# Encoder trunk in generator steps: one order list a layer, 512-column query/key projections, diff scores over 128 rows, norm and residual loads later

## The chip, the cores and the metric

The program runs on one core of one Trainium2 chip. A core has five engines with instruction queues of their own: TensorE (PE, matmuls; its weight loads are listed as PEld), VectorE (DVE), ScalarE (ACT), GpSimd (POOL) and SyncE (SP, which here only issues DMAs). The metric is the device time of one execution in microseconds (us). Before the change it is 1037.87 us, the median of three runs (1037.47 to 1038.59). All rows below come from one profiled execution of 1037.91 us, whose span from the first to the last instruction is 1035.7 us, so 2.2 us lie around the span; it stands 0.04 us from the median.

## The reference

Two layers of an encoder over 256 tokens of width 1024. Each layer projects x once into queries, keys, values and gates, runs three attention branches, merges them through sigmoid gates, and adds a feed-forward block. Cut to what matters:

```python
for l in range(DEPTH):                                   # DEPTH = 2
    h = x @ w_in[l]
    c_q, c_kv, k_pe, dq, dk, dv, mq, gate_pre = jnp.split(h, splits, axis=-1)
    o_mla  = _mla_branch(...)                            # 8 heads, low-rank q and kv
    o_diff = _diff_branch(dq, dk, dv, ...)               # 8 heads, two softmax maps each
    o_mem  = _mem_branch(mq, mem, mem_w_kv[l])           # 4 heads into 256 memory tokens
    merged = g0*(o_mla @ wb0) + g1*(o_diff @ wb1) + g2*(o_mem @ wb2)
    x = _layernorm(DEEPNORM_ALPHA * x + merged @ w_out[l], ln1_g[l], ln1_b[l])
    f = jnp.square(jax.nn.relu(x @ mlp_w1[l])) @ mlp_w2[l]
    x = _layernorm(DEEPNORM_ALPHA * x + f, ln2_g[l], ln2_b[l])

# diff branch: q, k are (b, s, 8 heads, 2 maps, 64); rope on the first 16 of 64
sc = jnp.einsum('bqhcd,bkhcd->bhcqk', qblk, k) * 64 ** -0.5
p  = softmax(sc);  w = p[:, :, 0] - lambda_full * p[:, :, 1];  o = w @ v
```

## The kernel before

Every operand of a matmul is split into a high and a low part, both in the type fp32r: `evac` (L129) writes the high part with ACT and the low part, the rest, with DVE, and `mm3` (L112) multiplies high x high, high x low and low x high as three matmuls into one PSUM tile. Weights come by `wload` (L93): one DMA of 512 KB on SP's queue into a `raw` tile, a cast on ACT (L104) and a subtraction on DVE (L105) into a `whl` tile. There are 6 `raw` and 8 `whl` tiles. PSUM has two rings of four tiles, `acc` and `sm`.

A layer is emitted as steps in the order of the string `ORDER` (L52). P0 to P3 are the diff projections of two heads each, D0 to D3 their attention, K, Q and M the memory branch, L, U and A the latent branch, g, h, e the gates and G, H, E the branch products. Then come `w_out`, a layer norm, the feed-forward block (`mlp1`, `mlp2`) and a second layer norm. A step is one Python call. The framework's scheduler then fixes each engine's order from all the instructions that were emitted; every engine runs its own queue strictly in that order and waits on semaphores.

The places that the change touches:

- `DiffProj` (L189) projects queries, keys and values of two heads as three pieces `i` of 256 columns each for two tiles `t` of 128 tokens. Queries and keys of a token tile share one PSUM tile, queries in columns 0 to 255 and keys in 256 to 511. `finish` copies that tile (L232), rotates it, transposes it (L240) and splits queries and keys with `evac` (L242).
- `diff_head` (L448) computes the scores of one head. A head has two maps of 64 dimensions, map 0 on partitions 0 to 63 and map 1 on 64 to 127, so each matmul (L458) uses 64 rows: 2 token tiles x 3 products x 2 maps, 12 a head, each over 256 columns. The two maps alternate.
- `ln_params` (L532) takes a `whl` tile for the norm's gain and bias; `xn` (L821) loads the residual. The second norm's load is emitted ahead of the feed-forward block (L862).
- For the first layer's P0 the kernel calls `first.both()` (L316): piece by piece, and within a piece both token tiles.

Of the kernel before, what the change touches and what calls it, by code (L numbers as in the profile page):

```python
# [43 lines left out]
BUFS = dict(raw=6, whl=8, whlx=4, att=12, o=6, pexp=4, natd=3, gt=4, fr=2, pT=2)  # L44
# [7 lines left out]
ORDER = "P0 T0 L0 K0 Q0 D0 U0 M0 P1 D1 M1 P2 D2 P3 g0 A0 G0 D3 g1 g2 A1 G1 A2 G2 g3 G3 h0 H0 h1 A3 h2 H1 e0 h3 H2 H3 e1 E0 e2 e3 E1 E2 E3"  # L52
CONST_W = 1700
# [3 lines left out]
def encoder_trunk(ctx: ExitStack, tc: tile.TileContext, x, mem, positions, w_in, b_gate,  # L57
# [34 lines left out]

    def wload(src, a, b, ring="whl"):  # L93
# [95 lines left out]
    class DiffProj:  # L189
# [12 lines left out]
        def proj(self, i, t):  # L202
            stage[0] = "diff_proj"
            if i == 2:
                if self.vv is None:
                    self.vv = acc_tile()
                d = self.vv[:, t * T:(t + 1) * T]
            else:
                if self.qk[t] is None:
                    self.qk[t] = acc_tile()  # L210
                d = self.qk[t][:, i * T:(i + 1) * T]
            for k in range(KD):
                w = self.weights(i, k // 4)
                xh, xl = xk(self.xT, k, t)
                mm3(d, xh, xl, w[0][:, k % 4], w[1][:, k % 4], k == 0, k == KD - 1)

        def step(self, t):
            for i in range(3):
                self.proj(i, t)

        def both(self):
            for i in range(3):
                for t in range(2):
                    self.proj(i, t)
            return self

        def finish(self):
            stage[0] = "diff_proj"
            nats = []
            for t in range(2):  # L230
# [39 lines left out]
    def mem_keys(l, mT, ptile):  # L270
        stage[0] = "mem_keys"
        K = []
        for hp in range(2):
            ws = [wload(wsrc(w_mkv[l], 4 * c, 4, hp * 256, 256), 4, 256) for c in range(2)]
# [12 lines left out]
        return K  # L287
# [28 lines left out]
    first.both()  # L316
# [112 lines left out]
    def attend_pair(q, k, rows):  # L429

        st = tmp.tile([P, 2, 2], F32, tag="st", bufs=4, name=nm("st"))
        pes = []
        for t in range(2):
            ps = sm_tile()
# [5 lines left out]
            pes.append(softmax_exp(ps, st, t))  # L440
        rc = tmp.tile([P, 2, 2], F32, tag="rc", bufs=4, name=nm("rc"))
# [4 lines left out]
        return [transpose_probs([pes[t][:, j, :] for t in range(2)]) for j in range(2)]  # L446

    def diff_head(l, q, k, j, vh, on):  # L448

        st = tmp.tile([P, 2, 2], F32, tag="st", bufs=4, name=nm("st"))  # L450
        pss = [sm_tile() for _ in range(2)]
        ks = slice(j * T, (j + 1) * T)
        for t in range(2):
# [6 lines left out]
        pes = [softmax_exp(pss[m], st, m) for m in range(2)]  # L460
        rc = tmp.tile([P, 2, 2], F32, tag="rc", bufs=4, name=nm("rc"))
# [4 lines left out]
        for t in range(2):  # L466
            V.scalar_tensor_tensor(pes[0][:, t, :], pes[1][:, t, :], rc[:, 1, t:t + 1], pes[0][:, t, :],
                                   ALU.mult, ALU.add)
        pT = transpose_probs([pes[0][:, t, :] for t in range(2)])
        po = sm_tile()  # L470
# [8 lines left out]
        ss = tmp.tile([P, 2], F32, tag="ss", bufs=4, name=nm("ss"))  # L479
        junk = tmp.tile([P, 384], F32, tag="junk", bufs=1, name=nm("junk"))  # L480
        for t in range(2):
            S.activation(junk[:, :P], on[:, t, :], AF.Square, accum_out=ss[:, t:t + 1])
        rs_ = tmp.tile([P, 2], F32, tag="rs", bufs=4, name=nm("rs"))
        G.tensor_tensor(rs_, ss, rc[:, 0, :], ALU.add)
        G.tensor_tensor(rs_, rs_, nhalf[:, :2], ALU.pow)
        for t in range(2):
            S.activation(on[:, t, :], on[:, t, :], AF.Copy, scale=rs_[:, t:t + 1])

# [8 lines left out]
    def relu_sq(ps):  # L497
        r = tmp.tile([P, 512], F32, tag="gt", bufs=BUFS["gt"], name=nm("relu"))
# [33 lines left out]
    def ln_params(g, b):  # L532
        gb = wp.tile([P, 2, D], F32, tag="whl", bufs=BUFS["whl"], name=nm("lnp"))
# [438 lines left out]
```

## Time and profile before

| What | Value |
|---|---|
| Median of three runs | 1037.87 us (1037.47 to 1038.59) |
| Profiled execution | 1037.91 us, span 1035.7 us |
| PE busy | 1018.0 us, 98% of the span, 6725 matmuls |
| PEld (weight loads) busy | 926.5 us, 89% |
| DVE busy | 723.6 us, 70% |
| ACT busy | 571.7 us, 55% |
| POOL busy | 54.6 us, 5% |
| DMA, main queue | 176.71 MB, 56.7% of 16 engines |
| Chain that ended last | PE 97%, DVE 1%, DMA 1% |

Busy time counts a moment once however many instructions of the engine are in flight then. Matmuls overlap: one is listed with 280 ns, while the next starts 120 ns behind it. What a matmul costs in a stream is therefore the distance from its start to the next start, and not its listed duration.

### The profile page before, as it was taken

Reading aid. Unit: us, or ns where it says so; the run is one execution under the profiler, and the core shown is the slowest. Engines: PE = TensorE matmul, PEld = TensorE weight load, DVE = VectorE, ACT = ScalarE, POOL = GpSimd, SP = SyncE. Lnnn points to the kernel's source line nnn. Section 1 sums busy time; section 2 is a strip of 40 time slices with the busy share of each in tenths; the row PEclk is TensorE's granted clock in tenths of the full one; section 3 lists DMA queues with packets and bytes.
Section 4 is the critical chain, followed back from the end, with each engine's and each line's share of the span. In section 5 each row is a group of like instructions: output and inputs, shape, how many; then the busy total and the mean of one; then the engine's idle time right before and its main releaser. Section 6 shows DMA issues by size and latency. Waiting matters only on the chain.

```text
span 1035.7 us, 17211 instructions
## 1 busy us (share of the span) xinstructions
PE 1018.0 (98%) x6725; PEld 926.5 (89%) x6725; DVE 723.6 (70%) x1095; ACT 571.7 (55%) x1054; POOL 54.6 (5%) x102
## 2 busy tenths in 40 slices
PE   7999999999999999999999999999999999999996
PEld 6989999999998888888889999999999978888885
DVE  5868778766869776556876777776677876556664
ACT  5857657657554554445625775666565625344540
POOL 0201000001000000000000210100000010000001
PEclk9999999999999999999999999999999999999999
DMA  8956444444558466666845864445455835755531
GB/s 295 337 161 173 134 123 145 141 123 125 173 181 274 143 203 190 193 187 183 252 128 186 237 163 124 133 132 142 122 147 160 265 122 166 240 163 183 183 102 41
DMA packets 132761, 178.11 MB, mean 172 GB/s; under 512 B 6028, under 2 KB 114632, under 8 KB 132680
## 3 DMA queue, kind: packets, MB, share of 16 engines
q1 hardware_dynamic: 132032, 176.71, 56.7%
q8 instruction: 53, 0.87, 0.4%
q10 hardware_dynamic: 648, 0.31, 0.1%
q14 instruction: 28, 0.23, 0.1%
HBM read 174.89 MB, written 2.10 MB: 171 GB/s over the span
## 4 chain that ended last, share of the span: by engine, by line
PE 97%; DVE 1%; DMA 1%; ACT 0%; SPq 0%; issue 0%; POOLq 0%; POOL 0%; DVEq 0%
PE mlp1.sm L121 11%; PE mlp2.acc L113 6%; PE mlp2.acc L115 6%; PE mlp2.acc L114 6%; PE mlp1.sm L123 5%; PE diff_proj.acc L113 5%; PE diff_proj.acc L114 5%; PE diff_proj.acc L115 5%; PE gate.acc L115 4%; PE gate.acc L113 4%; PE gate.acc L114 4%; PE branch.acc L114 4%; PE branch.acc L113 4%; PE branch.acc L115 4%; PE diff_att.sm L458 2%; PE diff_att.sm L474 2%
## 5 line engine op out<-in xcount | busy, mean ns | idle before, releaser
L105 DVE TENSOR_TENSOR mlp1.whl<-mlp1.raw,mlp1.whl 128x1024 fp32r<-128x1024 f32 x124 | 150.1, 1223 | 69.8 <-ACT mlp1.whl L104 67.8
L121 PE MATMUL mlp1.sm<-wout.xT,mlp1.whl 128*128 128x512 f32 x480 | 166.6, 397 | 0.0
L104 ACT CAST mlp1.whl<-mlp1.raw 128x1024 fp32r<-128x1024 f32 x124 | 127.8, 1049 | 62.2 <-PE mlp2.acc L115 23.6
L123 PE MATMUL mlp1.sm<-wout.xT,mlp1.whl 128*128 128x256 f32 x420 | 117.8, 280 | 0.0
L121 PEld LDWEIGHTS mlp1.sm<-wout.xT,mlp1.whl 128*128 128x128 f32 x480 | 87.0, 188 | 16.8
L113 PE MATMUL mlp2.acc<-mlp1.whl,mlp1.att 128*128 128x512 f32 x240 | 95.1, 396 | 0.0
L115 PE MATMUL mlp2.acc<-mlp1.whl,mlp1.att 128*128 128x512 f32 x240 | 94.2, 393 | 0.0
L114 PE MATMUL mlp2.acc<-mlp1.whl,mlp1.att 128*128 128x512 f32 x240 | 94.0, 392 | 0.0
L123 PEld LDWEIGHTS mlp1.sm<-wout.xT,mlp1.whl 128*128 128x128 f32 x420 | 79.3, 189 | 2.6
L105 DVE TENSOR_TENSOR gate.whl<-gate.raw,gate.whl 128x1024 fp32r<-128x1024 f32 x48 | 58.7, 1223 | 25.5 <-ACT gate.whl L104 24.0
L105 DVE TENSOR_TENSOR diff_proj.whl<-diff_proj.raw,diff_proj.whl 128x1024 fp32r<-128x1024 f32 x47 | 57.4, 1222 | 20.3 <-ACT diff_proj.whl L104 19.7
L494 ACT COPY mlp1.sum<-mlp1.sm 128x256 f32<-128x256 f32 x60 | 22.4, 373 | 87.2 <-PE mlp1.sm L121 87.2
L104 ACT CAST diff_proj.whl<-diff_proj.raw 128x1024 fp32r<-128x1024 f32 x47 | 49.3, 1050 | 27.0 <-PE diff_proj.acc L115 16.0
L104 ACT CAST gate.whl<-gate.raw 128x1024 fp32r<-128x1024 f32 x48 | 50.3, 1049 | 20.7 <-PE gate.acc L115 10.0
L113 PE MATMUL diff_proj.acc<-diff_proj.whl,mlp1.xT 128*128 128x256 f32 x192 | 54.8, 286 | 0.5 <-ACT mlp1.xT L131 0.5
L113 PE MATMUL gate.acc<-start.xT,gate.whl 128*128 128x256 f32 x192 | 55.0, 286 | 0.0
L113 PE MATMUL gate.acc<-mlp1.xT,gate.whl 128*128 128x256 f32 x192 | 55.0, 286 | 0.0
L115 PEld LDWEIGHTS mlp2.acc<-mlp1.whl,mlp1.att 128*128 128x128 f32 x240 | 45.1, 188 | 11.1
L114 PE MATMUL diff_proj.acc<-diff_proj.whl,mlp1.xT 128*128 128x256 f32 x192 | 55.0, 287 | 0.0
L115 PE MATMUL gate.acc<-start.xT,gate.whl 128*128 128x256 f32 x192 | 54.8, 285 | 0.0
L115 PE MATMUL gate.acc<-mlp1.xT,gate.whl 128*128 128x256 f32 x192 | 54.8, 285 | 0.0
L114 PE MATMUL gate.acc<-start.xT,gate.whl 128*128 128x256 f32 x192 | 54.6, 284 | 0.0
(360 smaller groups left out, 2952.1 us busy)
## 6 DMA issues: line engine op xcount, KB each, us to landing
mlp1.raw<-in_mlp_w_dram SPq DMA_DIRECT2D x124, 512.0 KB, 4.6
gate.raw<-in_w_in_dram SPq DMA_DIRECT2D x48, 512.0 KB, 3.8
diff_proj.raw<-in_w_in_dram SPq DMA_DIRECT2D x47, 512.0 KB, 4.6
branch.raw<-in_w_branch_dram SPq DMA_DIRECT2D x32, 512.0 KB, 3.6
wout.raw<-in_w_out_dram SPq DMA_DIRECT2D x16, 512.0 KB, 3.8
mem_keys.raw<-in_mem_w_kv_dram SPq DMA_DIRECT2D x8, 512.0 KB, 5.4
mem_vals.raw<-in_mem_w_kv_dram SPq DMA_DIRECT2D x8, 512.0 KB, 6.9
mq.raw<-in_w_in_dram SPq DMA_DIRECT2D x8, 512.0 KB, 5.4
```

The lines of the kernel that those rows point to most:

```text
L104: S.copy(out=hl[:, 0, :n], in_=raw[:, :n])
L105: V.tensor_tensor(hl[:, 1, :n], raw[:, :n], f32v(hl[:, 0, :n]), ALU.subtract)
L113: PE.matmul(ps, lhsT=lh, rhs=rh, start=start, stop=False)
L114: PE.matmul(ps, lhsT=lh, rhs=rl, start=False, stop=False)
L115: PE.matmul(ps, lhsT=ll, rhs=rh, start=False, stop=stop)
L121: PE.matmul(ps, lhsT=lh, rhs=r2, start=first, stop=last)
L123: PE.matmul(ps[:, 0, :], lhsT=ll, rhs=r2[:, 0, :], start=False, stop=False)
L458: PE.matmul(pss[m][:, t * T:(t + 1) * T], lhsT=q[rs, a, qs], rhs=k[rs, b, ks], start=i == 0, stop=i == 2)
L474: PE.matmul(po[:, t * T:(t + 1) * T], lhsT=pT[:, hl, kt * T + t * P:kt * T + (t + 1) * P], rhs=vh[:, :, kt * T + j * P:kt * T + (j + 1) * ...
L494: S.copy(out=d, in_=ps[:, 1, :])
```

## The change

The order string becomes one list a layer, and a step's name now stands in it as many times as the step has pieces: each step is a generator, and each mention emits its next piece. The order of the steps is the one of before, and all pieces of a step stand together. In the diff:

- Queries and keys of a diff group are projected together over 512 columns: `wload` gets two sources of 256 columns (two DMAs of 256 KB each) for two k-blocks, instead of one of 256 columns for four. For the first layer's P0 the loop is now over token tiles, and each takes all queries, keys and values (`first.step(t)`).
- `turn` lays the operands of the scores out over 128 partitions: map `m` of `q2` holds the high part of the queries on its 64 partitions and the low part on the other 64; `kh` holds the high part of the keys on both halves and `kl` the low part on both. Two matmuls over 128 rows then give all four products (before: three products). `turn` has 6 ACT and 6 DVE instructions on 64 partitions where `finish` had 2 and 2 on 128.
- Each step of `diff_att` works on both heads in turn (scores of both, transposes of both, products of both).
- The norm parameters have a tile of their own (`lnp`), the residual and norm loads are issued behind the last weight load of the step before them (`issue_after`), and the second norm's load is emitted behind the feed-forward block. The gates have tiles of their own, and the values of `mla_up` are split in one piece instead of two.

```diff
-ORDER = "P0 T0 L0 K0 Q0 D0 U0 M0 P1 D1 M1 P2 D2 P3 g0 A0 G0 D3 g1 g2 A1 G1 A2 G2 g3 G3 h0 H0 h1 A3 h2 H1 e0 h3 H2 H3 e1 E0 e2 e3 E1 E2 E3"
-CONST_W = 1700
+ORDER = (
...
-            nc.sync.dma_start(out=rv, in_=src)
+            loads[:] = [nc.sync.dma_start(out=rv, in_=src).ins]
...
-                o = (O_DQ, O_DK, O_DV)[i] + self.g * 256
-                self.ws[i, c] = wload(wsrc(w_in[self.l], 4 * c, 4, o, 256), 4, 256)
+                o = self.g * 256
+                self.ws[i, c] = (wload(wsrc(w_in[self.l], 4 * c, 4, O_DV + o, 256), 4, 256) if i else
+                                 wload([wsrc(w_in[self.l], 2 * c, 2, b + o, 256) for b in (O_DQ, O_DK)], 2, 512))
...
+        def queries_keys(self, t, cs=range(4)):
...
+            for c in cs:
+                w = self.weights(0, c)
+                for k in range(2 * c, 2 * c + 2):
+                    xh, xl = xk(self.xT, k, t)
+                    mm3(self.qk[t], xh, xl, w[0][:, k % 2], w[1][:, k % 2], k == 0, k == KD - 1)
...
+            rows = (slice(0, 64), slice(64, 128))
+            q2, kh, kl = slot(), slot(), slot()
+            for m in range(2):
+                a, b = rows[m], rows[1 - m]
+                S.activation(q2[a, m, :], pst[0][a, :], AF.Copy, scale=0.125)
+                V.scalar_tensor_tensor(q2[b, m, :], pst[0][a, :], 0.125, f32v(q2[a, m, :]),
+                                       ALU.mult, ALU.subtract)
+                S.copy(out=kh[a, m, :], in_=pst[1][a, :])
+                S.copy(out=kh[b, m, :], in_=pst[1][a, :])
+                V.tensor_tensor(kl[a, m, :], pst[1][a, :], f32v(kh[a, m, :]), ALU.subtract)
+                V.tensor_tensor(kl[b, m, :], pst[1][a, :], f32v(kh[a, m, :]), ALU.subtract)
+            return q2, (kh, kl), self.vh
...
-    first.both()
+    for t in range(2):
+        first.step(t)
...
-        for t in range(2):
-            qs = slice(j * T + t * P, j * T + (t + 1) * P)
-            for i, (a, b) in enumerate(((0, 0), (0, 1), (1, 0))):
-                for m in range(2):
-                    rs = slice(m * 64, (m + 1) * 64)
-                    PE.matmul(pss[m][:, t * T:(t + 1) * T], lhsT=q[rs, a, qs], rhs=k[rs, b, ks],
-                              start=i == 0, stop=i == 2)
+        for m in range(2):
+            for t in range(2):
+                qs = slice(j * T + t * P, j * T + (t + 1) * P)
+                d = pss[m][:, t * T:(t + 1) * T]
+                PE.matmul(d, lhsT=q[:, m, qs], rhs=kh[:, m, ks], start=True, stop=False)
+                PE.matmul(d, lhsT=q[:, m, qs], rhs=kl[:, m, ks], start=False, stop=True)
...
-        gb = wp.tile([P, 2, D], F32, tag="whl", bufs=BUFS["whl"], name=nm("lnp"))
-        nc.sync.dma_start(out=gb[:, 0, :], in_=g.partition_broadcast(P))
-        nc.sync.dma_start(out=gb[:, 1, :], in_=b.partition_broadcast(P))
+        gb = act.tile([P, 2, D], F32, tag="lnp", bufs=1, name=nm("lnp"))
+        with tc.issue_after(loads[0]):
+            nc.sync.dma_start(out=gb[:, 0, :], in_=g.partition_broadcast(P))
+            nc.sync.dma_start(out=gb[:, 1, :], in_=b.partition_broadcast(P))
...
+            heads = [diff_head(l, qT, kT, j, vh, ons[j]) for j in range(2)]
+            for _ in range(3):
+                for h in heads:
+                    next(h)
+                    yield
...
-            nc.sync.dma_start(out=xn, in_=x_in[t])
+            with tc.issue_after(loads[0]):
+                nc.sync.dma_start(out=xn, in_=x_in[t])
```

Three places show what becomes of the order. The first is SP's queue at the start of the program: behind the weights of P0 (`raw`) stood the memory tokens (`memn`) and between them the two residual tiles (`xn`).

```order
L102 DMA diff_proj.raw_237<-in_w_in_dram 128x4x256
L102 DMA diff_proj.raw_254<-in_w_in_dram 128x4x256
L253 DMA load_memT.memn_382<-in_mem_dram 128x1024
L822 DMA branch.xn_3886<-in_x_dram 128x1024
L822 DMA branch.xn_3888<-in_x_dram 128x1024
L253 DMA load_memT.memn_384<-in_mem_dram 128x1024
L102 DMA latent.raw_418<-in_w_in_dram 128x2x288
```

Now the same stretch reads:

```order
L107 DMA diff_proj.raw_168<-in_w_in_dram 128x4x256
L107 DMA diff_proj.raw_185<-in_w_in_dram 128x4x256
L285 DMA load_memT.memn_347<-in_mem_dram 128x1024
L285 DMA load_memT.memn_349<-in_mem_dram 128x1024
L107 DMA latent.raw_383<-in_w_in_dram 128x2x288
```

The residual tiles are gone from the start; they now stand behind the last branch weights of the layer.

The second place is PE in the first layer's P0, where the first weight chunk is used up and the second one begins. `acc_123` and `acc_153` are the query/key tiles of the two token tiles, `whl_103` and `whl_138` the first two chunks. Before:

```order
L113 MATMUL diff_proj.acc_153<-start.whl_103,start.xT_82 128x256
L114 MATMUL diff_proj.acc_153<-start.whl_103,start.xT_82 128x256
L115 MATMUL diff_proj.acc_153<-start.whl_103,start.xT_82 128x256
L113 MATMUL diff_proj.acc_123<-diff_proj.whl_138,start.xT_83 128x256
L113 MATMUL diff_proj.acc_153<-diff_proj.whl_138,start.xT_83 128x256
```

Now `acc_124` and `acc_202` are those two tiles, `acc_167` the values, and the chunks in the order of loading are `whl_104`, 134, 146, 158 (queries and keys) and 170 (values). The 19th matmul over 512 columns and what follows it:

```order
L119 MATMUL diff_proj.acc_124<-diff_proj.whl_146,start.xT_83 128x512
L120 MATMUL diff_proj.acc_124<-diff_proj.whl_146,start.xT_83 128x512
L118 MATMUL diff_proj.acc_124<-diff_proj.whl_158,start.xT_83 128x512
L118 MATMUL diff_proj.acc_167<-diff_proj.whl_170,start.xT_82 128x256
L118 MATMUL diff_proj.acc_202<-start.whl_104,start.xT_82 128x512
```

PE took both token tiles from a chunk before it needed the next one; now it comes to the fourth and the fifth chunk with the first token tile alone, and only then takes up the second token tile with the first chunk.

The third place is PE in the scores of the second diff group of layer 0. `sm_1443` and `sm_1444` are the two maps of its first head; `acc_1667` belongs to P2 and `sm_1215` to the memory branch. Before:

```order
L113 MATMUL mem_att.sm_1215<-mem_att.pT_1204,mem_vals.att_800 128x256
L458 MATMUL diff_att.sm_1443<-diff_proj.att_1423,diff_proj.att_1422 128x256
L113 MATMUL diff_proj.acc_1667<-diff_proj.whl_1635,start.xT_82 128x256
L114 MATMUL diff_proj.acc_1667<-diff_proj.whl_1635,start.xT_82 128x256
L115 MATMUL diff_proj.acc_1667<-diff_proj.whl_1635,start.xT_82 128x256
L113 MATMUL diff_proj.acc_1667<-diff_proj.whl_1635,start.xT_82 128x256
L458 MATMUL diff_att.sm_1443<-diff_proj.att_1423,diff_proj.att_1422 128x256 x5
L114 MATMUL diff_proj.acc_1667<-diff_proj.whl_1635,start.xT_82 128x256
```

Now (`sm_1335`, `sm_1336` the first head, `sm_1360` the second, `acc_1513` P2):

```order
L118 MATMUL diff_proj.acc_1513<-diff_proj.whl_1541,start.xT_83 128x512
L497 MATMUL diff_att.sm_1335<-diff_proj.att_1319,diff_proj.att_1317 128x256
L496 MATMUL diff_att.sm_1335<-diff_proj.att_1318,diff_proj.att_1317 128x256
L497 MATMUL diff_att.sm_1335<-diff_proj.att_1319,diff_proj.att_1317 128x256
L119 MATMUL diff_proj.acc_1513<-diff_proj.whl_1541,start.xT_83 128x512
L120 MATMUL diff_proj.acc_1513<-diff_proj.whl_1541,start.xT_83 128x512
L118 MATMUL diff_proj.acc_1513<-diff_proj.whl_1541,start.xT_83 128x512
L496 MATMUL diff_att.sm_1336<-diff_proj.att_1318,diff_proj.att_1317 128x256
L496 MATMUL diff_att.sm_1360<-diff_proj.att_1318,diff_proj.att_1317 128x256
```

The scores still stand among matmuls of other steps, and are as often split, but they are now matmuls over 128 rows like their neighbours.

## Rows read from the trace of the kernel before

**Rows 1.** The page: span, then busy us (share of span) and instructions.

```profile
span 1035.7 us, 17211 instructions
PE 1018.0 (98%) x6725; PEld 926.5 (89%) x6725; DVE 723.6 (70%) x1095; ACT 571.7 (55%) x1054; POOL 54.6 (5%) x102
```

**Rows 2.** The two largest of PE's four waits: us in total, times, longest.

```profile
PE start.sm L175 <- DMA start.x<-in_x_dram: 7.1, 2, 4.0
PE mlp1t.sm L524 <- DVE mlp1t.fr L501: 1.4, 1, 1.4
```

**Rows 3.** Groups by form: line, shapes, count, busy, mean ns: the score matmuls.

```profile
L458 PE MATMUL diff_att.sm<-diff_proj.att,diff_proj.att 64*128 64x256 f32 x192 | 23.7, 303 | 0.0
```

**Rows 4.** Timeline of PE (start, us, count): one whole head's scores; a split one.

```profile
82.18 0.39 PE L121 MATMUL mq.acc<-start.xT,mq.whl 128*128 128x512 f32 x1
82.50 0.98 PE L458 MATMUL diff_att.sm<-diff_proj.att,diff_proj.att 64*128 64x256 f32 x12
83.41 0.44 PE L113 MATMUL uq.acc<-uq.whl,latent.att 128*128 128x384 f32 x1
83.69 0.34 PE L114 MATMUL uq.acc<-uq.whl,latent.att 128*128 128x384 f32 x1
83.87 0.34 PE L115 MATMUL uq.acc<-uq.whl,latent.att 128*128 128x384 f32 x1
...
125.54 0.28 PE L113 MATMUL diff_proj.acc<-diff_proj.whl,start.xT 128*128 128x256 f32 x1
125.75 0.85 PE L458 MATMUL diff_att.sm<-diff_proj.att,diff_proj.att 64*128 64x256 f32 x5
126.53 0.39 PE L114 MATMUL diff_proj.acc<-diff_proj.whl,start.xT 128*128 128x256 f32 x1
126.76 0.28 PE L115 MATMUL diff_proj.acc<-diff_proj.whl,start.xT 128*128 128x256 f32 x1
```

**Rows 5.** Timeline of PE: streams over 256 and 512 columns, first and last of each.

```profile
13.38 0.41 PE L114 MATMUL diff_proj.acc<-start.whl,start.xT 128*128 128x256 f32 x1
13.59 0.41 PE L115 MATMUL diff_proj.acc<-start.whl,start.xT 128*128 128x256 f32 x1
...
16.25 0.28 PE L114 MATMUL diff_proj.acc<-diff_proj.whl,start.xT 128*128 128x256 f32 x1
...
22.01 0.28 PE L114 MATMUL diff_proj.acc<-diff_proj.whl,start.xT 128*128 128x256 f32 x1
...
845.63 0.39 PE L114 MATMUL mlp1t.sm<-mlp1t.whl,wout.xT 128*128 128x512 f32 x1
...
849.26 0.39 PE L115 MATMUL mlp1t.sm<-mlp1t.whl,wout.xT 128*128 128x512 f32 x1
...
1015.00 0.39 PE L114 MATMUL mlp2.acc<-mlp1.whl,mlp1.att 128*128 128x512 f32 x1
...
1026.90 0.39 PE L114 MATMUL mlp2.acc<-mlp1.whl,mlp1.att 128*128 128x512 f32 x1
```

**Rows 6.** Timelines of DVE and ACT in P0: fifth chunk's subtraction, a table load.

```profile
18.71 1.23 DVE L105 TENSOR_TENSOR diff_proj.whl<-diff_proj.raw,diff_proj.whl 128x1024 fp32r<-128x1024 f32 x1 [0.22 <-ACT diff_proj.whl L104]
...
18.84 1.28 ACT L400 ACT_TABLE_LOAD   x1
```

**Rows 7.** The chain in order of time: the transposes at the end of P0.

```profile
30.57 0.87 PE diff_proj.acc L240 x8
```

**Rows 8.** Groups by form on DVE and ACT: splits of queries, and 64 against 128 partitions.

```profile
L135 DVE SCALAR_TENSOR_TENSOR diff_proj.att<-diff_proj.acc,diff_proj.att 128x512 fp32r<-128x512 f32 x8 | 5.5, 684 | 1.1 <-ACT diff_proj.att L134 1.1
L134 ACT ACTIVATE diff_proj.att<-diff_proj.acc 128x512 fp32r<-128x512 f32 x8 | 4.8, 601 | 2.1 <-PE diff_proj.acc L240 2.1
L781 DVE TENSOR_TENSOR mla_att.total<-mla_att.sm,mla_att.part 64x256 f32<-64x256 f32 x16 | 6.7, 420 | 4.4 <-ACT mla_att.part L779 4.3
L783 DVE TENSOR_TENSOR mla_att.o<-mla_att.total,mla_att.o 128x256 fp32r<-128x256 f32 x8 | 3.3, 414 | 0.0
```

**Rows 9.** Busy us by stretch (from:to, length, then PE, PEld, DVE, ACT, POOL): layer 0.

```profile
82.00:170.00 88.00, 88.00 (x695) 84.20 (x694) 67.59 (x127) 58.55 (x139) 7.73 (x16) 1.00 0.52 145
```

More of the change, by code (lines that the diff above doesn't have):

```diff
@@ L91, in f32v @@
         return ap.bitcast(F32)
+    loads = []
     def wload(src, a, b, ring="whl"):
@@ L151, in encoder_trunk, with scalars @@
     carve = icarve = carver(const.tile([P, CONST_W], F32, name="consts"))
+    def scalars():
+        return carver(tmp.tile([P, 32], F32, tag="sc", bufs=BUFS["sc"], name=nm("sc")))
+    junk = carve(512)
+    free_gates = [carve(512) for _ in range(BUFS["gt"])]
     ident = carve(P)
@@ L233, in finish, with keep_values, turn @@
                 rope(nat.rearrange("p (n d) -> p n d", n=8)[:, :, :ROT_D], cos_d, sin_d, t, 8, ROT_D)
-                nats.append(nat)
-            qT, kT, vh = slot(), slot(), slot()
-            for i, d in enumerate((qT, kT)):
+                self.nats.append(nat)
+        def keep_values(self):
+            self.vh = slot()
+            evac(self.vh[:, 0, :], self.vh[:, 1, :], self.vv)
+        def turn(self):
+            stage[0] = "diff_proj"
+            pst = []
+            for i in range(2):
                 ps = acc_tile()
@@ L427, in transpose_probs, with attend_pair @@
         return pT
-    def attend_pair(q, k, rows):
-        st = tmp.tile([P, 2, 2], F32, tag="st", bufs=4, name=nm("st"))
+    def attend_pair(q, k, rows, name, pTs):
+        take = scalars()
+        st, rc = take(2, 2), take(2, 2)
         pes = []
         for t in range(2):
+            stage[0] = name
             ps = sm_tile()
@@ L439, in attend_pair @@
                     True, True)
-            pes.append(softmax_exp(ps, st, t))
-        rc = tmp.tile([P, 2, 2], F32, tag="rc", bufs=4, name=nm("rc"))
+            pes.append(softmax_exp(ps, take(2), st, t))
+            yield
+        stage[0] = name
         V.reciprocal(rc, st)
@@ L539, in layernorm @@
         stage[0] = "layernorm"
-        bs = tmp.tile([P, 2, 6], F32, tag="bs", bufs=2, name=nm("bs"))
+        take = scalars()
+        bs, mv, rs_ = take(2, 6), take(2), take(1)
         for h in range(2):
@@ L559, in encoder_trunk, with project, diff_att @@
         wi = w_in[l]
-        def diff_att(g, qkv):
-            stage[0] = "diff_att"
-            qT, kT, vh = qkv
-            ons = []
-            for j in range(2):
-                on = tmp.tile([P, 2, P], F32, tag="on", bufs=3, name=nm("on"))
-                diff_head(l, qT, kT, j, vh, on)
-                ons.append(on)
+        omem, odiff, omla, mq, qkv, gates, mla = [], [], [], [], {}, {}, {}
+        merged, mhl = [None] * 4, [None] * 4
+        if l == 0:
+            K, Vt = [], []
+        def project(n):
+            if n == 0:
+                p = first
+                if l > 0:
+                    p.step(1)
+                p.rotate()
+                p.keep_values()
+                yield
+            else:
+                p = DiffProj(l, n, xT)
+                for c in range(4):
+                    for t in range(2):
+                        p.queries_keys(t, [c])
+                    if c % 2:
+                        if c == 3:
+                            p.rotate()
+                        yield
+                for t in range(2):
+                    p.values(t)
+                p.keep_values()
+                yield
+            qkv[n] = p.turn()
+        def diff_att(g):
+            qT, kT, vh = qkv[g]
+            ons = [tmp.tile([P, 2, P], F32, tag="on", bufs=3, name=nm("on")) for _ in range(2)]
+            heads = [diff_head(l, qT, kT, j, vh, ons[j]) for j in range(2)]
+            for _ in range(3):
+                for h in heads:
+                    next(h)
+                    yield
+            stage[0] = "diff_att"
             ps = sm_tile()
@@ L587, in gate @@
             for j in range(2):
+                stage[0] = "gate"
                 for k in range(KD):
@@ L609, in branch @@
             for j in range(2):
+                stage[0] = "branch"
                 for k in range(nk):
@@ L753, in mla_att @@
             stage[0] = "mla_att"
-            q, k = (act.tile([P, 2, 512], F32R, tag="att", bufs=BUFS["att"], name=nm("mqk")) for _ in range(2))
+            qn, kfull, vm = mla["qn"], mla["kfull"], mla["vm"]
+            q, k = slot(), slot()
             for src, d, sc in ((qn, q, 96.0 ** -0.5), (kfull, k, None)):
@@ L850, in encoder_trunk @@
             if t == 1 and l + 1 < DEPTH:
-                K = mem_keys(l + 1, memT, sm_tile)
+                K = []
+                for _ in mem_keys(l + 1, memT, sm_tile, K):
+                    pass
             elif t == 1:
```

187 lines of the change are left out of this document (86 added, 101 removed).

## The prediction

> **What bounds the kernel now.** I read the page first, then PE's waits, the groups by form, the timeline of PE where the change touches it, the chain in order of time, and last the load of DVE and ACT in the stretches with diff work.
>
> The page says that PE is busy for 1018.0 of 1035.7 us [rows 1], and its two largest waits come to 7.1 us for the first x tiles and 1.4 us in the feed-forward block [rows 2]. Almost nothing else holds PE up: the time is the sum of the distances between matmul starts. So each matmul that goes is worth its distance, and each wait that appears is paid in full. DVE (70%) and ACT (55%) have room over the whole span [rows 1]; whether they have it in the diff stretches is the question below.
>
> The distances: a stream over 256 columns takes 48 steps from 16.25 to 22.01, that is 0.120 us each. A stream over 512 columns takes 16 steps from 845.63 to 849.26, 0.227 each, in a place like the new one (one token tile of x against moving weights), and 51 steps from 1015.00 to 1026.90, 0.233 each, in another [rows 5]. So one wide matmul in place of two narrow ones saves 0.007 to 0.013 us.
>
> **The change part by part.**
>
> *Scores.* 192 matmuls over 64 rows become 128 over 128 rows, each over 256 columns. The 192 are busy for 23.7 us [rows 3], a time in which overlaps count once. They stand in 32 unbroken blocks (counted in the timeline), and each block costs something at its edges. For the whole head at 82.50, the matmul ahead starts at 82.18, and 0.32 us pass where a step over 512 columns takes 0.23; the first one behind it needs 0.28 where the next of its kind needs 83.87 - 83.69 = 0.18 [rows 4]. That is 0.09 ahead and 0.10 behind. From one neighbour to the other it is 83.69 - 82.18 = 1.51; less 0.23 and 0.18 for the neighbours, the twelve cost 1.10, which is their busy 0.98 and 0.12. The split one agrees: 126.76 - 125.54 = 1.22, less two steps of 0.12, makes 0.98 for only five matmuls, listed with 0.85 [rows 4]. So I count busy time plus 0.12 a block: 23.7 + 32 x 0.12 = 27.5 us. The 128 new ones have the shape of their neighbours and need no such edges: 128 x 0.120 = 15.3 us. The saving is **12.2 us**. As the lower bound I keep the edges, as though the change of tile and not of the row count made them: 15.3 + 32 x 0.19 = 21.4, a saving of 6.1.
>
> Here rows show edges at every block. The Trainium skill ("TensorEngine Tiling (Array Packing)", Key Properties) states that a change of the tiling mode drains TensorE, and by that rule too they go with the 64-row form. Its section Theoretical Speedup speaks against the change: with 64 or fewer rows two matmuls may run at once, up to twice as fast. The trace shows that pairing (23.7 us busy for 192 listed with 303 ns), so it is a rival below.
>
> *Queries and keys.* 8 groups x 2 token tiles x 8 k-blocks x 3 products = 384 wide matmuls replace 768 narrow ones. The 48 of the first P0 are in the next item; 336 are left, with 336 x 0.007 = 2.3 to 336 x 0.013 = 4.4 us. The row nearest in form is the one with 0.227; I take 0.228: 336 x 0.012 = **4.0 us**.
>
> The Trainium skill ("TensorE: Matmul & The Clock Gate", Back-to-back issue gap) gives a matmul its columns at 2.4 GHz and about 2.5 ns. By that the pair would save only 2.5 ns, 0.8 us over the 336, and the sum would come out 3.2 us higher. The rows of this case stand above it for 256 columns (0.120) and for 512 (0.227), and have the larger difference, so I go by them.
>
> *The start.* P0 of layer 0 used to take both token tiles from a chunk before the next was due. Now PE uses all chunks for the first tile and then returns to chunk one. Up to the fifth chunk (the first values) it has only 19 wide matmuls to do. That chunk's low part was done at 18.71 + 1.23 = 19.94 [rows 6]. If it comes no sooner, PE waits for it and has 5 + 24 wide and 48 narrow matmuls left: 29 x 0.228 + 48 x 0.120 = 12.4 us, ending at 32.3. The transposes of that group began at 30.57 [rows 7]. So **+1.7 us**, the 48 wide ones included. Down to -2, since 1 MB of residual loads leaves the start of SP's queue, and the loads might come sooner; up to +4, since two more table loads of the kind of 1.28 us [rows 6] stand early on ACT, each chunk of queries and keys is now two DMAs, and PE, with waits in between, may run longer at the half rate (1.2 GHz) that the 0.21 us between 13.38 and 13.59 show for 256 columns [rows 5].
>
> *The turn.* Each of the 8 groups gets 4 more ACT and 4 more DVE instructions of 512 columns. That they have 64 partitions doesn't make them shorter: a DVE operation on 64 partitions takes 420 ns, its like on 128 takes 414 [rows 8]. So DVE gains 4 x 0.68 = 2.7 us and ACT 4 x 0.60 = 2.4 a group, 22 and 19 us in all. What hides them is PE's other work: scores stand among projections of the next group, the memory and the latent branch. In the stretch 82 to 170 DVE is busy for 67.6 of 88 us [rows 9]. With three more turns it would be 75.7, in a stretch that gets some 6 us shorter: 92%. That leaves little slack, and DVE also makes the low parts of the weights, 1.22 us a chunk, behind which a late turn puts the next chunk. Bounds: nothing, or all 8 in full, 22 us. I take **+2.0 us**, near nothing, as before shows almost no PE wait with the same chain at 77% DVE.
>
> *Residual and norm loads.* They are 2 x 2 residual tiles and the norm pairs, on SP's queue behind the last weights of the step ahead; nobody needs them until the layer norm. The weights of the end are there long before use, so a queue that moves by some 4 us stays hidden: 0. If that cover were gone, each norm would pay one such load, the 4.0 us that the x tile's longer wait has [rows 2], at most.
>
> *Generator steps.* The order of the steps is that of before. Pieces of both heads in turn bring no instruction; the transposes stay in number. 0, with what they could cost inside the +2.0.
>
> The sum goes against the profiled execution's 1037.91 us (span 1035.7, 2.2 around it), 0.04 from the median: 1037.9 - 12.2 - 4.0 + 1.7 + 2.0 = **1025.4 us**.
>
> **The rivals.**
>
> 1. *More is gained.* The start costs nothing and the turns hide fully: 1037.9 - 12.2 - 4.0 = 1021.7, with wide matmuls and loads at their better ends 1020. For it: PE waits little anywhere [rows 2]. Against it: the count of matmuls before the fifth chunk.
>
> 2. *The edges stay, or the turns hold PE up in part.* Scores save 6.1 instead of 12.2: 1031.5; or the turns cost 1 us a group instead of a quarter: 1031.4. For it: DVE at 92%. Against it: edges stand where the row count changes, and steps over 128 rows elsewhere have none.
>
> 3. *Slower by the turns.* The longer chain of evacuations ends last for every group, since scores of a group can't start before all six pairs of writes are done. At its full price of 22 us the time is 1023.4 + 22 = 1045; it decides the sign from 14.5 us, that is 1.8 us a group. For it: the turn's ACT and DVE steps follow each other. Against it: PE has a next group's projection between.
>
> 4. *Packing is worth more than the edges.* If pairs of 64-row matmuls are what counts, 96 pairs at the 0.120 of one step are 11.5 us, and 128 matmuls cost 3.8 more, not 12.2 less: 1037.9 + 3.8 - 4.0 + 1.7 + 2.0 = 1041.4. For it: the 12 of a whole head start in pairs. Against it: their 1.10 us are more than eight steps of 0.120, and in 32 blocks for 16 heads most are split.
>
> 5. *The change is not what it says:* the wide projections run at 0.240, no faster than two narrow ones: 1029.4.
>
> **How the numbers follow.** The forecast has a chance of 0.60 with 1022 to 1029 as its own range, rival 5 included in its upper end; more gained 0.13; rival 2 0.17; rival 3 at a price that reaches the sign 0.06, and rival 4 0.04. A measurement of this kernel tells 0.2%, about 2 us, from no change. Rivals 3 and 4 end slower, 0.07 of their 0.10 beyond the 2 us; partial prices land within it with 0.04: faster 0.89, same 0.04, slower 0.07. The range runs from 1020 (rival 1) to 1034, which takes in rival 2 and leaves out 3 and 4.
>
> **What would show it.** Right: no score block with an edge above 0.05 us, 128 score matmuls at 0.120; wide projections at 0.227 to 0.233; the first P0's transposes at 31 to 33 us after a wait of PE for the fifth chunk's low part; DVE at about 90% in the diff stretches with PE waits of a few us on `turn`'s tiles. Wrong: PE waits on `turn` above 1.8 us in every group (rival 3), score steps above 0.15 us (rivals 2 and 4), a first P0 that ends after 35 us, or new waits of PE for weights outside of the diff stretches.

## The result, and the profile after

The changed kernel takes **1022.6 us** (median of 4 runs, 1022.21 to 1023.78) against 1037.8; the ratio is 0.9854, its 95% interval 0.9837 to 0.9871. That lies in the range and 2.8 us under the forecast of 1025.4. The profiled execution took 1022.91 us. Its page answers [rows 1]:

```profile
span 1021.1 us, 16419 instructions
PE 998.9 (98%) x6277; PEld 903.2 (88%) x6277; DVE 742.1 (73%) x1119; ACT 593.0 (58%) x1080; POOL 52.9 (5%) x102
```

PE is still what the time hangs on. DVE and ACT are busy for 18.5 and 21.3 us more, near the 22 and 19 that the turn was counted with.

The scores of the first diff group in PE's timeline (start, us, line), which answers the whole-head block of [rows 4]:

```profile
83.57 0.40 PE L126 MATMUL mq.acc<-start.xT,mq.whl 128*128 128x512 f32 x1
83.80 0.28 PE L496 MATMUL diff_att.sm<-diff_proj.att,diff_proj.att 128*128 128x256 f32 x1
83.92 0.28 PE L497 MATMUL diff_att.sm<-diff_proj.att,diff_proj.att 128*128 128x256 f32 x1
...
85.59 0.28 PE L497 MATMUL diff_att.sm<-diff_proj.att,diff_proj.att 128*128 128x256 f32 x1
85.71 0.34 PE L118 MATMUL uq.acc<-uq.whl,latent.att 128*128 128x384 f32 x1
85.89 0.34 PE L119 MATMUL uq.acc<-uq.whl,latent.att 128*128 128x384 f32 x1
```

The 0.09 us ahead of a block and the 0.10 behind it are gone: 83.57 to 83.80 is a plain wide step, 85.71 to 85.89 a plain one over 384 columns, and 16 matmuls between them take 1.91 us. The Trainium skill ("TensorEngine Tiling (Array Packing)", Key Properties) states that a change of the tiling mode drains TensorE. The trace fits that: edges at the blocks of 64 rows before, none here.

All waits of PE (us in total, times, longest), against [rows 2]:

```profile
PE start.sm L187 <- DMA start.x<-in_x_dram: 7.9, 2, 4.3
PE mlp1t.sm L563 <- DVE mlp1t.fr L540: 1.5, 1, 1.5
PE diff_att.sm L454 <- ACT uq.nat L800: 1.1, 1, 1.1
PE load_memT.acc L118 <- ACT branch.att L697: 0.8, 1, 0.8
PE diff_proj.acc L119 <- DVE diff_proj.whl L110: 0.8, 1, 0.8
PE mlp1t.sm L118 <- ACT wout.xT L136: 0.5, 2, 0.2
PE diff_proj.acc L118 <- ACT mlp1.xT L136: 0.5, 2, 0.2
PE load_memT.acc L120 <- DVE branch.att L698: 0.5, 1, 0.5
PE diff_proj.acc L118 <- ACT diff_proj.whl L109: 0.3, 1, 0.3
```

The new ones are few: 1.1 us in layer 1's D0 (at the transposes of its probabilities), 1.3 in `w_out` of layer 0 (ACT splits `branch.att` behind casts that wait for weights), 1.1 in the first P0. None stands at the tiles that the turn writes.

Sorting the distances between the starts of all matmuls of both traces gives where the 14.7 us between the last matmuls (1027.13 and 1012.42) come from. An excess is what a single distance has beyond the usual one of its shape:

| Part | Before, us | After, us | Difference |
|---|---|---|---|
| Score matmuls with the edges of their blocks (32, then 26) | 27.4 | 15.3 | -12.1 |
| Up to the transposes of the first P0 | 30.4 | 32.0 | +1.6 |
| Queries and keys behind it: 672 x 0.1197, then 336 x 0.227 | 80.4 | 76.3 | -4.2 |
| All steps over 512 columns, beyond 0.227 each | 10.5 | 6.1 | -4.4 |
| All steps over 256 columns, beyond 0.1197 each | -2.6 | -1.4 | +1.2 |
| Excesses over 0.2 us behind P0 | 3.2 | 6.4 | +3.2 |
| Rest | | | 0.0 |

The wide steps of queries and keys stand in their row with 0.227 us, their commonest step; their mean is 0.229, and the difference is in the row below. That row was in no term of the prediction. It lies mostly in `mlp2`, whose code and order did not change. Groups by form, the three products of `mlp2` before:

```profile
L113 PE MATMUL mlp2.acc<-mlp1.whl,mlp1.att 128*128 128x512 f32 x240 | 95.1, 396 | 0.0
L115 PE MATMUL mlp2.acc<-mlp1.whl,mlp1.att 128*128 128x512 f32 x240 | 94.2, 393 | 0.0
L114 PE MATMUL mlp2.acc<-mlp1.whl,mlp1.att 128*128 128x512 f32 x240 | 94.0, 392 | 0.0
```

and after, with two places 53 steps apart in its last stream (timeline):

```profile
L118 PE MATMUL mlp2.acc<-mlp1.whl,mlp1.att 128*128 128x512 f32 x240 | 93.5, 389 | 0.0
L120 PE MATMUL mlp2.acc<-mlp1.whl,mlp1.att 128*128 128x512 f32 x240 | 93.4, 389 | 0.0
...
1000.41 0.39 PE L118 MATMUL mlp2.acc<-mlp1.whl,mlp1.att 128*128 128x512 f32 x1
...
1012.42 0.39 PE L120 MATMUL mlp2.acc<-mlp1.whl,mlp1.att 128*128 128x512 f32 x1
```

Each got 3 to 7 ns shorter, and 53 steps in 12.01 us are 0.227 each, where [rows 5] has 0.233.

### The profile page after: what moved, and what is told of

It is laid out like the page before. It is cut to its first block, busy times and chain, and to the rows that moved or that the text cites. A ratio compares the mean times of both kernels' runs of the same rounds, so it can differ in the third digit from the quotient of the medians.

```text
span 1021.1 us, 16419 instructions
## 1 busy us (share of the span) xinstructions
PE 998.9 (98%) x6277; PEld 903.2 (88%) x6277; DVE 742.1 (73%) x1119; ACT 593.0 (58%) x1080; POOL 52.9 (5%) x102
## 4 chain that ended last, share of the span: by engine, by line
PE 94%; DMA 2%; ACT 2%; DVE 1%; issue 0%; SPq 0%; POOLq 0%; POOL 0%; DVEq 0%; ACTq 0%
PE mlp1.sm L126 11%; PE branch.acc L120 6%; PE branch.acc L119 6%; PE branch.acc L118 6%; PE mlp2.acc L118 6%; PE mlp2.acc L119 6%; PE mlp2.acc L120 6%; PE mlp1.sm L128 5%; PE diff_proj.acc L119 5%; PE diff_proj.acc L118 5%; PE diff_proj.acc L120 5%; PE diff_att.sm L515 1%; PE mq.acc L126 1%; PE latent.acc L120 1%; PE latent.acc L118 1%; PE latent.acc L119 1%
## 5 line engine op out<-in xcount | busy, mean ns | idle before, releaser
L118 PE MATMUL mlp2.acc<-mlp1.whl,mlp1.att 128*128 128x512 f32 x240 | 93.5, 389 | 0.0
L120 PE MATMUL mlp2.acc<-mlp1.whl,mlp1.att 128*128 128x512 f32 x240 | 93.4, 389 | 0.0
L119 PE MATMUL mlp2.acc<-mlp1.whl,mlp1.att 128*128 128x512 f32 x240 | 93.4, 389 | 0.0
L110 DVE TENSOR_TENSOR branch.whl<-branch.raw,branch.whl 128x1024 fp32r<-128x1024 f32 x56 | 68.4, 1221 | 26.5 <-ACT branch.whl L109 26.1
L109 ACT CAST branch.whl<-branch.raw 128x1024 fp32r<-128x1024 f32 x56 | 58.8, 1051 | 32.8 <-PE branch.acc L120 19.7
L110 DVE TENSOR_TENSOR diff_proj.whl<-diff_proj.raw,diff_proj.whl 128x1024 fp32r<-128x1024 f32 x51 | 62.1, 1222 | 15.1 <-ACT diff_proj.whl L109 13.0
L109 ACT CAST diff_proj.whl<-diff_proj.raw 128x1024 fp32r<-128x1024 f32 x51 | 53.9, 1061 | 18.2 <-PE diff_proj.acc L120 11.0
L120 PEld LDWEIGHTS mlp2.acc<-mlp1.whl,mlp1.att 128*128 128x128 f32 x240 | 45.1, 188 | 9.5
L119 PEld LDWEIGHTS mlp2.acc<-mlp1.whl,mlp1.att 128*128 128x128 f32 x240 | 45.1, 188 | 9.4
L118 PEld LDWEIGHTS mlp2.acc<-mlp1.whl,mlp1.att 128*128 128x128 f32 x240 | 45.1, 188 | 8.8
L118 PE MATMUL diff_proj.acc<-diff_proj.whl,mlp1.xT 128*128 128x512 f32 (+1 forms) x128 | 44.0, 345 | 0.5 <-ACT mlp1.xT L136 0.5
L119 PE MATMUL diff_proj.acc<-diff_proj.whl,mlp1.xT 128*128 128x512 f32 (+1 forms) x128 | 43.2, 338 | 0.0
L120 PE MATMUL diff_proj.acc<-diff_proj.whl,mlp1.xT 128*128 128x256 f32 (+1 forms) x128 | 43.1, 340 | 0.0
L119 PE MATMUL diff_proj.acc<-diff_proj.whl,start.xT 128*128 128x256 f32 (+1 forms) x124 | 42.1, 340 | 0.8 <-DVE diff_proj.whl L110 0.8
L118 PE MATMUL diff_proj.acc<-diff_proj.whl,start.xT 128*128 128x256 f32 (+1 forms) x124 | 42.0, 341 | 0.3 <-ACT diff_proj.whl L109 0.3
```

The costliest lines, as they stand in the source:

```text
L109: S.copy(out=hl[:, 0, :n], in_=raw[:, :n])
L110: V.tensor_tensor(hl[:, 1, :n], raw[:, :n], f32v(hl[:, 0, :n]), ALU.subtract)
L118: PE.matmul(ps, lhsT=lh, rhs=rh, start=start, stop=False)
L119: PE.matmul(ps, lhsT=lh, rhs=rl, start=False, stop=False)
L120: PE.matmul(ps, lhsT=ll, rhs=rh, start=False, stop=stop)
```

## The experiments

Times are medians; the kernel before ran at 1037.96, 1037.55 and 1037.81 us beside the three groups of runs.

**Why `mlp2` got faster.** The diff has a new width of the constants' tile. In before, the tiles behind it started 32 bytes past a multiple of 64; in after, all tiles start at one. The traces hold no addresses: these places, and the distances below, are worked out from the layout of the tiles. Four runs change this width alone, and each engine's order of instructions in their traces is the same as without the change; one lengthens the weight tiles.

```diff
-CONST_W = 1700                          # before
+CONST_W = 1712                          # before_aligned
+CONST_W = 1728                          # before_apart_0
+CONST_W = 1696                          # before_apart_128
-CONST_W = 2304 + 512 * BUFS["gt"]       # after
+CONST_W = 2304 + 512 * BUFS["gt"] + 8   # after_32_off
```

> The kernel before with the constants' tile widened from 1700 to 1712 numbers, so that every SBUF tile behind it starts at a multiple of 64 bytes instead of 32 bytes past one; each engine's order of instructions stays. Theory A, a stationary operand 32 bytes off costs about 6 ns per matmul over 512 columns: 912 such matmuls times 5.8 ns are 5.3 us, so 1032.5 us, and the steps of mlp2 fall from 0.233 to 0.227 everywhere. Rival B, the faster steps of after come from its order and addresses play no part: 1037.8 us, steps as before.

Measured: 1031.65 us (ratio 0.9941, 0.9929 to 0.9954). Theory A seemed right, but the mean step was 0.229 and not 0.227.

> The changed kernel with the constants' tile 8 numbers (32 bytes) wider, so that every SBUF tile behind it starts 32 bytes past a multiple of 64; each engine's order stays. Theory A: 1536 matmuls over 512 columns with a plain moving operand, 5.8 ns each, 8.9 us: 1031.5 us. Rival B: 1022.6 us.

Measured: 1022.65 us, no change. Theory A fell: shifted all together, tiles off a multiple of 64 cost nothing.

> The changed kernel with weight tiles that are 32 bytes longer, so that about half of them start 32 bytes past a multiple of 64 while x and the probabilities mostly don't. In 720 matmuls over 512 columns only the moving operand is off, in 48 only the stationary one. Theory A (the stationary operand's address counts): 0.227 us for the 720 and 0.233 for the 48. Rival A2 (the moving one's counts): the other way round, and some 4 us more in total.

Here the tiles' own width was changed:

```diff
-        hl = wp.tile([P, 2, 1024], F32R, tag=ring, ...)
+        hl = wp.tile([P, 2056], F32R, tag=ring, ...)
+        hl = hl[:, :2048].rearrange("p (h n) -> p h n", h=2)
```

Measured in one run: 1022.94 us, with 0.233 us for the moving operand off alone (mean of 663 steps), 0.233 for the stationary one alone (46) and 0.231 for neither. So neither address counts by itself. What sorts the steps of these traces is the distance between the start of the moving operand (whose columns are streamed) and that of the next matmul's stationary operand (the weights that are loaded), modulo 256 bytes: 96 in before, 64 in before_aligned, 0 in after. Two more runs set it.

> The kernel before with the constants' tile of 1728 numbers: in the 861 matmuls over 512 columns that were off, the moving operand and the next stationary one now start at the same place modulo 256 bytes (96 apart in before, 64 apart in the run with 1712). Order of instructions as before. Theory A2, the distance of the two modulo 256 bytes counts: 0.227 us for all steps over 512 columns, 5 us less there and up to 1 us more in steps over 256 columns, 1033.5 us. Rival A, each tile's own multiple of 64 bytes counts: as with 1712 numbers, 1031.7 us with steps of 0.229.

Measured: 1033.48 us (ratio 0.9956, 0.9942 to 0.9969), as forecast.

> The kernel before with the constants' tile of 1696 numbers: every tile at a multiple of 64 bytes, but the 861 pairs 128 bytes apart modulo 256. Theory A2: 0.232 us a step as in the half-shifted weights, 1036.5 to 1038 us. Rival A: as with 1712 numbers, 1031.7 us.

Measured: 1037.11 us (0.9992, 0.9983 to 1.0), though every tile is at a multiple of 64. Rival A is out. The groups of the two runs, first 0 apart, then 128:

```profile
L113 PE MATMUL mlp2.acc<-mlp1.whl,mlp1.att 128*128 128x512 f32 x240 | 93.5, 389 | 0.0
L115 PE MATMUL mlp2.acc<-mlp1.whl,mlp1.att 128*128 128x512 f32 x240 | 93.4, 389 | 0.0
```

```profile
L113 PE MATMUL mlp2.acc<-mlp1.whl,mlp1.att 128*128 128x512 f32 x240 | 94.4, 393 | 0.0
L115 PE MATMUL mlp2.acc<-mlp1.whl,mlp1.att 128*128 128x512 f32 x240 | 94.4, 393 | 0.0
```

Mean steps at each distance (in the kernel before, of the pairs that the width moves):

| Distance modulo 256 bytes (run) | Mean step, 512 columns | Mean step, 256 columns |
|---|---|---|
| 0 (after; before_apart_0) | 227.5 ns; 226.9 | 119.2 ns; 119.3 |
| 64 (before_aligned; its 256-column ones at 192) | 229.1 | 115.7 |
| 96 (before; its 256-column ones at 160) | 233.4 | 117.9 |
| 128 (before_apart_128) | 232.5 | 118.8 |

So about 4.3 us of the 15.2 come from where the tiles lie, 1037.81 - 1033.48, and they lie in steps of code that the change left alone. That the places do it is shown, since nothing else differs between these runs. The distance as the rule is their best reading: it forecast the last two times. Whether the next matmul's stationary operand counts or the same matmul's, and whether 256 bytes is the right period, they do not tell apart. The place with the lowest total was 64, not 0 (1031.65 against 1033.48), because of the steps over 256 columns; it was not tried on the changed kernel.

**The scores alone, and what hides the turn.**

```diff
             q2, kh, kl = slot(), slot(), slot()      # finish of before: the 12 writes of the change's turn
...
+                PE.matmul(d, lhsT=q[:, m, qs], rhs=kh[:, m, ks], start=True, stop=False)
+                PE.matmul(d, lhsT=q[:, m, qs], rhs=kl[:, m, ks], start=False, stop=True)
```

> The kernel before with the scores over 128 rows alone (operands laid out as in the change, projections, loads and addresses as before). Theory: the 32 blocks of 64-row matmuls and their edges go, 27.4 us become 15.3, and the longer turn costs 0 to 2 us: 1025.7 to 1027.7 us. Rival, edges stay at every block: 1031.7 us. Rival, the longer turn is paid in full: 1047 us.

Measured: 1041.72 us (1038.28 to 1044.64; ratio 1.0033, 1.002 to 1.0045): a little slower than before, and beyond the theory. The scores themselves behave (15.2 us with edges in its profile). What comes back is waiting, and more of it from run to run: the mean granted clock is 0.996 in the run of 1038.28 us and 0.991 in that of 1044.64. The profiled run took 1039.61, 2.1 under the median. PE's largest wait in it, and what follows in the timeline:

```profile
98.21 0.99 PE L486 MATMUL diff_att.sm<-diff_proj.att,diff_att.pT 128*128 128x256 f32 x7
102.83 0.35 PE L113 MATMUL diff_proj.acc<-diff_proj.whl,start.xT 128*128 128x256 f32 x1 [3.63 <-DVE ukv.att L132]
...
105.33 0.41 PE L114 MATMUL diff_proj.acc<-diff_proj.whl,start.xT 128*128 128x256 f32 x1
105.55 0.41 PE L115 MATMUL diff_proj.acc<-diff_proj.whl,start.xT 128*128 128x256 f32 x1
105.76 0.41 PE L113 MATMUL diff_proj.acc<-diff_proj.whl,start.xT 128*128 128x256 f32 x1
```

Its windows (from:to, length, busy us of PE, PEld, DVE, ACT, POOL, then the granted clock, DMA share, GB/s):

```profile
95.00:100.00 5.00, 4.20 (x26) 3.55 (x24) 4.96 (x11) 4.22 (x14) 0.00 (x0) 1.00 0.77 212
100.00:105.00 5.00, 2.17 (x15) 2.21 (x16) 4.34 (x12) 3.17 (x15) 1.32 (x4) 0.91 0.65 169
105.00:110.00 5.00, 5.00 (x35) 5.00 (x35) 0.69 (x1) 1.25 (x2) 0.00 (x0) 0.75 0.13 44
110.00:115.00 5.00, 5.00 (x45) 5.00 (x44) 4.25 (x5) 2.68 (x9) 0.29 (x2) 1.00 0.44 112
```

DVE is full from 95 to 100 us, and PE waits until DVE has split the latent values. Then the steps are 0.21 us instead of 0.12, the 1.2 GHz level, until the clock is back: 0.09 x 5 + 0.25 x 5 = 1.7 us more. A wait of 3.6 us here cost 5.3.

> The kernel before with scores over 128 rows, and with the values of the latent branch split in 4 pieces of 256 columns instead of 8 of 128 (as in the change). Theory: ACT and DVE were full between 92 and 103 us, and PE's wait of 3.8 us there and the half clock behind it (1.7 us lost) go in part or in whole: 1036 to 1039 us, against 1041.7 without this edit. Rival: the wait comes from the turn alone, 1041.7 us; what covers it in the changed kernel is then the order of its smaller steps.

```diff
-                    for j in range(2):
-                        evac(vv[:, 4 * n + j:4 * n + 4:2, j, :], vv[:, 4 * n + j:4 * n + 4:2, 1 - j, :],
-                             pv[:, j::2, 64:128])
+                    evac(vv[:, 4 * n:4 * n + 4, 0, :], vv[:, 4 * n:4 * n + 4, 1, :], pv[:, :, 64:128])
```

Measured: 1035.37 us (0.9982, 0.9973 to 0.9991), 6.4 less than without it, the wait and its clock both gone:

```profile
100.00:105.00 5.00, 5.00 (x44) 5.00 (x44) 4.84 (x10) 3.67 (x14) 1.68 (x4) 1.00 0.53 130
105.00:110.00 5.00, 5.00 (x45) 5.00 (x44) 3.05 (x6) 2.98 (x6) 0.00 (x0) 1.00 0.75 208
```

Four splits of 416 ns on DVE had replaced eight of 279 a layer, half the instructions. Against 1037.8 - 12.1 = 1025.7, 9.7 us are still lost; the remaining waits stand at the latent tiles, at the gates and at `mla_att.o` ahead of the branch products. In the changed kernel they are not there. Which of its other edits removes them is not shown: the generator steps (heads in turn, smaller pieces), the wide projections, the tiles of their own for gates and norms, and the later loads were not run apart.

> The changed kernel with each of the 12 instructions of the turn issued twice (the same values are written again). Theory, the turn is hidden beside PE's other work but for the waits of D0: 0 to 3 us more, 1022.6 to 1026 us. Rival, its time is paid as the scores wait for it: 8 groups times 6 times 0.6 us are 29 us, 1051 us.

```diff
-            for m in range(2):
+            for m in (0, 1, 0, 1):
```

Measured: 1043.04 us (1.0044, 1.0031 to 1.0058), 20.4 more. Twelve writes more a group take some 29 us of ACT and 33 of DVE beside it, and two thirds of it show. Its largest wait behind the start, of 4.5 us, has the same tail as above. PE's timeline and the windows:

```profile
43.67 0.33 PE L120 MATMUL latent.acc<-latent.whl,start.xT 128*128 128x384 f32 x1
43.84 0.33 PE L118 MATMUL latent.acc<-latent.whl,start.xT 128*128 128x384 f32 x1
...
49.60 0.69 PE L118 MATMUL latent.acc<-latent.whl,start.xT 128*128 128x384 f32 x1 [4.55 <-ACT load_memT.nat L747]
50.08 0.53 PE L119 MATMUL latent.acc<-latent.whl,start.xT 128*128 128x384 f32 x1
50.40 0.53 PE L120 MATMUL latent.acc<-latent.whl,start.xT 128*128 128x384 f32 x1
```

```profile
45.00:50.00 5.00, 0.45 (x2) 0.40 (x2) 4.87 (x11) 3.50 (x9) 2.61 (x4) 0.79 0.49 145
50.00:55.00 5.00, 5.00 (x17) 5.00 (x17) 4.35 (x11) 3.21 (x4) 0.00 (x0) 0.53 0.01 3
```

Behind the wait a step takes 0.32 us instead of 0.17. The cover in the changed kernel holds one turn and not two; my theory of 0 to 3 us is wrong here, the rival nearer.

**The wide projections, undone.**

```diff
+                d = self.qk[t][:, c // 2 * T:(c // 2 + 1) * T]
+                for k in range(4 * (c % 2), 4 * (c % 2) + 4):
...
+                    mm3(d, xh, xl, w[0][:, k % 4], w[1][:, k % 4], k == 0, k == KD - 1)
```

> The changed kernel with queries and keys of the diff branch projected over 256 columns again (768 matmuls in place of 384, one DMA of 512 KB a chunk); all else as changed. Theory: 384 times (0.239 - 0.227) are 4.6 us more, 1027.2 us; by 0.233 a wide step it would be 2.3 more, 1024.9. Rival, wide matmuls bring nothing: 1022.6 us.

Measured: 1024.99 us, 2.4 more than after. Behind the first P0 the steps cost 3.9 us more (672 x 0.1197 less 336 x 0.227 is 4.2, and what lies beside these paces is 0.3 less), but the narrow form has 1.1 us less in excesses over 0.2 us, and 0.8 less around transposes. Most of the 1.1 is the wait in `w_out`, 0.8 us of excess here and 1.6 in the changed kernel; no run shows that the wide form makes it longer.

**Start and loads.**

> The changed kernel with the first layer's P0 in the order of before: of each weight chunk both token tiles, then the next chunk. Theory, the order by token tiles makes PE wait for chunks: P0 ends 1.0 to 1.4 us earlier, 1021.4 us. Rival, the start is bound by when the weights land and split whatever the order: 1022.6 us.

```diff
-    for t in range(2):
-        first.step(t)
+    for c in range(4):
+        for t in range(2):
+            first.queries_keys(t, [c])
+    for t in range(2):
+        first.values(t)
```

Measured: 1021.39 us (0.9837, 0.9823 to 0.985), 1.2 under the changed kernel: as forecast, and the fastest of all. But PE does not wait less in its P0. Its one wait there is longer than the changed kernel's 0.8 and 0.3:

```profile
PE diff_proj.acc L119 <- DVE diff_proj.whl L110: 2.0, 1, 2.0
```

It is for the second chunk's low part and ends at 17.30 us, with 34 wide matmuls of P0 still to do; the changed kernel's, for the third chunk's, ends at 18.13 with 35 to do. So P0's transposes begin at 30.92 us instead of 31.98. The size of the theory came out, its reason did not: which chunk is awaited, and when its low part is done, decides.

> The changed kernel with the residual tiles' loads no longer held behind the last branch weights. Theory, loads of the residual are hidden in either place: 1022.6 us within 0.5. Rival, at the start they take the DMA queues from the weights of P0: 1 to 3 us more there.

```diff
-            with tc.issue_after(loads[0]):
-                nc.sync.dma_start(out=xn, in_=x_in[t])
+            nc.sync.dma_start(out=xn, in_=x_in[t])
```

Measured: 1022.2 us, within 0.5 of after. The place of these loads is worth nothing that these runs can tell. The place of the norm loads was not run.

> The changed kernel with P0 of the first layer by weight chunk and with the residual loads not held back. Theory: the two gains add, 1021.4 - 0.4 = 1021.0 us. Rival: early residual loads delay the chunks of P0, which is now faster and needs them sooner: 1022 us or more.

Measured: 1022.74 us. The two do not add, and the rival's number came out; which of the waits of its start does it is left open.

## Why the prediction was right, point by point

- **What bounds it.** Right: PE at 98% before and after, and each matmul taken away was worth its distance.
- **Scores, -12.2.** Measured -12.1. Counting block edges from both neighbours was what made the term right: the listed busy time alone, 23.7 less 15.3, would have given 8.4. Rival 4 (packing) fell with the edges, and so did the lower bound that kept them. The gain comes out only with the turn covered: alone in the kernel before, the new scores made it slower.
- **Queries and keys, -4.0.** Too large: 2.4 by the run that undoes it. The step distance was near (0.227 as the commonest step, 0.229 as the mean, so 3.5 to 4.2 us), and rival 5 fell. What took the rest stands as waits and transposes in the traces; its cause is open.
- **Start, +1.7.** Measured +1.6, and 1.2 by the run that restores the order. The size was right by luck, as the place was not. PE did not wait for the fifth chunk's low part: it waited for the third's, and then went on with the second token tile. The old order does not spare PE a wait either.

PE in the first P0, timeline, and the chain in order of time where [rows 7] stood:

```profile
16.87 0.51 PE L118 MATMUL diff_proj.acc<-diff_proj.whl,start.xT 128*128 128x512 f32 x1 [0.29 <-ACT diff_proj.whl L109]
18.13 0.50 PE L119 MATMUL diff_proj.acc<-diff_proj.whl,start.xT 128*128 128x512 f32 x1 [0.75 <-DVE diff_proj.whl L110]
...
32.15 0.22 PE diff_proj.acc L259 x2
```

- **The turn, +2.0.** Excesses grew by 3.2, of which the listed rows give 1.1 in D0 and 1.3 in `w_out`. The part in `w_out` stands behind casts that wait for weights; nothing shows that the turn causes it, and new waits for weights outside of the diff stretches were among my signs of being wrong. PE waits on no tile of the turn, and DVE stands at 84% (72.33 of 86 us) in the first layer's diff stretch and not at 92%:

```profile
79.00:165.00 86.00, 85.89 (x539) 77.52 (x538) 72.33 (x133) 65.63 (x146) 7.15 (x16) 1.00 0.55 154
```

  So the term was near partly by luck, and its reason only half right: I named PE's other work as the cover, but with the same turn in the kernel before it cost 1041.72 - 1025.7 = 16 us. The cover is made by other edits of the change. The undivided latent values were worth 6.4 us of it in the kernel before; what makes the rest is open. I had given the smaller steps nothing, and the undivided values no term at all. Rival 3 was therefore the live danger, at 2.0 us a group there, above the 1.8 from which it decides.
- **Residual and norm loads, 0.** Right for the residual loads, within 0.4 us; the norm loads were not run apart.
- **What was missing.** Some 4.3 us from the places of the tiles. I had both ends of it in [rows 5], 0.227 and 0.233, and took them as a spread of what a wide step costs; one was a pair of tiles 0 apart, the other 96 apart. The diff line of `CONST_W` stood in front of me. This term alone is more than the 2.8 us by which the forecast was too high; the miss is no larger because queries and keys, counted 1.6 us too high, and the excesses, counted 1.2 too low, made up for a part of it.

## What to carry to other kernels

Where one engine is full, count what an edit takes from its stream by start distances, the edges at both neighbours with it. A stage's cover is part of the change: price an added evacuation by the part alone, and look at which other edits make room for it. When untouched code gets faster, compare where its tiles lie before explaining it by the order.

## What the runs showed of the hardware that was not expected

- Start distances of matmuls over 512 columns with fp32r operands depend on where the tiles lie. Sorted by the distance between the moving operand and the next stationary one they are 227 ns at 0 modulo 256 bytes, 229 at 64, 232 to 233 at 96 and 128. Over 256 columns the order is another: 119 ns at 0, 116 at 192. In `mlp1`, where matmuls over 512 and 256 columns alternate, the step over 512 columns stays at 234 to 235 ns in before, after and the four runs that set the width. That PE loads the next weights while it streams the present columns can be seen in the trace (PEld is busy for 88% of the span and PE for 98%); that the two reads meet there is a reading of it and not shown.
- None of these reaches the 216 ns that the Trainium skill ("TensorE: Matmul & The Clock Gate", Back-to-back issue gap) gives for 512 columns by its formula for an isolated matmul, or the 131 ns that it gives for a sustained stream. The measurement decides: 226.9 is the best mean here.
- A wait of PE of 3.6 us was followed by 1.7 us of lost clock, one of 4.5 us by 0.47 x 5 = 2.4 us (what the clock lost from 45 to 50 fell almost wholly into the wait and cost little), both at the 1.2 GHz level. Behind the waits of up to 1.5 us in the changed kernel the granted clock stays at 1.00.
